# The prompt's compression units placed in the first sample pair's products, the head's constants in one transfer, and the instruction orders written anew

## The chip, the cores and the metric

The kernel runs on one core of a Trainium2 chip. The metric is the device time of one execution, in microseconds. The time before is the median of three runs. Beside them stands one profiled execution, from which every duration below is taken.

## The reference

One layer of a decoder is computed for a prompt group of 512 tokens and, with the same weights, for 8 decode samples of one token each, whose past of 1024 tokens lies in paged caches. Everything is float32.

```python
shift, scale, gate = jnp.split(jax.nn.silu(c) @ w_ada + b_ada, 3, axis=-1)
h = x * (1.0 + scale[:, None, :]) + shift[:, None, :]
parts = jnp.split(h @ w_in, np.cumsum(IN_WIDTHS)[:-1], axis=-1)
...
o_a = nsa_attention(...)    # compressed blocks, top-16 selected blocks, a window
o_b = moba_attention(...)   # top-3 past blocks by q . mean(k), and the own block
y_a = (o_a.reshape(bsz, t, NSA_WIDTH) * jax.nn.silu(a_z)) @ w_up_a
y_b = (o_b.reshape(bsz, t, MOBA_WIDTH) * jax.nn.silu(b_z)) @ w_up_b
mixed = (jax.nn.sigmoid(m_a) * y_a + jax.nn.sigmoid(m_b) * y_b) @ w_out
x_new = layer_norm(DEEPNORM_ALPHA * x + gate[:, None, :] * mixed, ln_g, ln_b)
```

The part that the change is about is the compression. Blocks of 32 rows, 16 apart, of the raw keys and values go with a position term through a small two-layer network, once for the prompt's own rows (31 blocks a head) and once for each sample's cache (63 blocks a head):

```python
def compress(kseq, pos_emb, w1, b1, w2, b2):
    ...
    blk = kseq[:, idx] + pos_emb[None, None, :, None, :]
    blk = blk.transpose(0, 1, 3, 2, 4).reshape(bsz, n, g, CMP_LEN * dh)
    return jax.nn.gelu(blk @ w1 + b1) @ w2 + b2
```

## The kernel before, in words

**Numbers.** Prompt and samples are handled together as 520 columns of transposed activations, in two halves of 260 (`HB`). Every float32 operand of a large product is split into a high and a low part of a reduced type, and each product is made of three: high by high, low weights by high, high weights by low. The high part is a cast on ACT, the low part a subtraction (`lo`, L367) on DVE or POOL. `LO_ENG` gives the turns of the two by three short patterns.

**The start.** SP issues all loads, at most eight in flight. `cT` (72 columns, the conditioning vectors), `bT` (16, the biases of shift and scale) and `cst` (141, small constants) are three transfers (L640 to L643). The eight blocks of `ada_ss`, the weights of shift and scale, come in 16 halves of 0.52 MB (`load_ada`, L565), and eight rows of x, 0.27 MB each (`load_x`, L550). Rows 0 to 3 go to buffers shared with later work (`ev`, `z`, `tmp`, `ev`), rows 4 to 7 to four buffers of their own (`xr`). For each row j, `ada` makes shift and scale on PE, and `ada_h` makes the modulated row: its high part `hTh` by one activation on ACT (512 columns) and its low part `hTl` by a multiply and a subtraction on DVE. The products of the first three groups of columns of w_in (`kc`, `vc`, `ks`, weights in `kd`, `v2`, `kl`) are added up row by row as the rows arrive (`early_mm`).

**The fills and the compression.** Then `dense` makes the other columns of w_in, 24 or 48 products of 260 columns for each half (`d<-hTh,hl` and `d<-hTl,hl`; the gates `ag` with weights of only 64 columns). Their weights pass through a ring: `raw` from memory, `hl` after the split. Between them stands the compression, `phis`. First comes `phi_prompt`: the prompt's own `kc` and `vc` rows are ordered into a tile `u` as 64 units with two columns of the position term behind them, and 48 products of 66 columns (`s<-u,w1h` and `s<-u,w1l`: 2 for keys and values, 8 slices, 3 parts) give the hidden layer, `gelu` follows, and `second` makes the second layer. Then `phi_pair` does the same for four pairs of samples, with 256 columns, from eight chunks `craw` of the cache, each of which is cast and subtracted into `u` (L1022 and L367). `u` has two buffers. What the network adds for the position term and bias, `cc`, is got from the last two columns of the prompt's products, so the prompt has to go through ahead of the first pair's `gelu`.

**What follows** is the same before and after but for its order: the decode samples' attention, the prompt's attention, the gates and up projections, the output projection, and the layer norm behind it.

**The order.** The program is traced in one order and then each engine's instructions are put into another one by `line_up`, from a table written out for each engine (`QUEUES`). A second set of tables (`SLOTS`) says for each pool which buffer the next tile gets. Nothing is decided by a scheduler at run time: an engine takes its next instruction and waits until its operands are there.

## Time and profile before

| | |
|---|---|
| runs | 604.09, 603.15, 602.0 us; median 603.15 |
| profiled execution | 605.51 us, of which the span of its trace is 603.8 |
| mean granted clock of PE in it | 0.991 |
| instructions of PE, DVE, ACT, POOL | 4721, 824, 688, 317 |
| bytes moved | 124.82 MB, mean 207 GB/s |
| chain that ended last | PE 79%, DVE 6%, DMA 5%, ACT 3%, POOL 2%, issue 2%, SP's queue 2% |

A row of the timeline has the start in us from the span's start, the duration, the engine, the line, the operation, "out<-in", the tile's shape, and how many like it follow one another ("x2"). In square brackets stands the idle time ahead of it and what ended that. Matmuls overlap, so the duration of one is longer than the distance from its start to the next start; the distance says what one costs. SPq is SP's queue of DMA issues; there the duration is that of issuing, with what holds up the issue. A row of the busy times by stretches has the stretch, its length, and for PE, PEld, DVE, ACT and POOL the busy time with the number of instructions, then the granted clock, the share of the DMA engines that was busy, and GB/s. A row of the groups has the count, the busy time and the mean ns of one, then the idle time ahead with its main releaser. PEld is the loading of weights, which overlaps PE.

### The profile page before, as it was taken

To read this page: it belongs to the slowest core of one execution; us is meant where nothing else is said; L and a number is where in the kernel's file an instruction comes from. 1 tells how busy PE (TensorE), PEld (TensorE's weight loads), DVE (VectorE), ACT (ScalarE), POOL (GpSimd) and SP (SyncE) were. 2 spreads that over 40 slices of the span, in tenths; PEclk is the share of its full clock that TensorE was granted. 3 is DMA by queue.
4 is the path that set the end of the run, shared out by engine and by line. 5 is a ranking of instruction groups with operands and counts; after the bars stand their busy time and mean duration, and the time that the engine had idled before them with its cause. 6 is when DMAs were issued, how large, how long until landed. Compare 5 with 4: busy or idle time off the path is not lost.

```text
span 603.8 us, 13227 instructions
## 1 busy us (share of the span) xinstructions
PE 588.1 (97%) x4721; PEld 504.0 (83%) x4721; DVE 293.2 (49%) x824; ACT 291.3 (48%) x688; POOL 271.5 (45%) x317
## 2 busy tenths in 40 slices
PE   7999999999999999999999999999999999999994
PEld 4789999999997888878768899987878697989773
DVE  1556534334374664644363545676421245334187
ACT  2457565635546546634446454575534134233343
POOL 0222567563433724351446728346361455354406
PEclk9998899999999999999999999999999999999998
DMA  8995465811665574466968635822997996332403
GB/s 300 401 362 169 111 195 162 277 36 36 185 183 166 186 246 144 161 234 240 370 226 324 246 122 197 279 104 57 325 399 245 374 347 222 106 117 89 188 1 141
DMA packets 63955, 124.82 MB, mean 207 GB/s; under 512 B 8402, under 2 KB 26258, under 8 KB 63378
## 3 DMA queue, kind: packets, MB, share of 16 engines
q1 hardware_dynamic: 62482, 119.79, 58.6%
q0 software_dynamic: 1408, 4.20, 1.8%
q8 instruction: 37, 0.61, 0.4%
q14 instruction: 28, 0.23, 0.1%
HBM read 114.37 MB, written 9.58 MB: 205 GB/s over the span
## 4 chain that ended last, share of the span: by engine, by line
PE 79%; DVE 6%; DMA 5%; ACT 3%; POOL 2%; issue 2%; SPq 2%; POOLq 0%; ACTq 0%; DVEq 0%
PE d L351 47%; PE s L351 12%; PE e L351 7%; PE o L351 5%; PE pt L354 5%; PE pt L351 2%; SPq L357 2%; DMA raw<-w_cols 2%; DMA u<-ada_ss 1%; DMA raw<-ada_g 1%; DVE bn L1762 1%; DMA raw<-mobv 1%; POOL p L1243 1%; DVE xt L1758 1%; POOL u L367 1%
## 5 line engine op out<-in xcount | busy, mean ns | idle before, releaser
L351 PE MATMUL d<-hTh,hl 128*128 128x260 f32 (+1 forms) x1392 | 266.4, 288 | 0.7 <-POOL hl L367 0.5
L351 PEld LDWEIGHTS d<-hTh,hl 128*128 128x128 f32 (+1 forms) x1392 | 217.1, 189 | 5.0 <-issue 1.7
L351 PE MATMUL d<-hTl,hl 128*128 128x260 f32 (+1 forms) x704 | 199.7, 284 | 0.0
L351 PEld LDWEIGHTS d<-hTl,hl 128*128 128x128 f32 (+1 forms) x704 | 132.5, 188 | 0.0
L367 POOL TENSOR_TENSOR hl<-raw,hl 128x512 fp32r<-128x512 f32 x57 | 77.3, 1356 | 113.8 <-ACT hl L447 91.4
L447 ACT CAST hl<-raw 128x512 fp32r<-128x512 f32 (+1 forms) x111 | 68.0, 617 | 51.4 <-PE d L351 43.9
L1241 ACT ACTIVATE p<-s,sm 128x256 f32<-128x256 f32 (+3 forms) x96 | 50.6, 529 | 71.5 <-DVE sm L1238 47.7
L1243 POOL TENSOR_SCALAR p<-p,sm,gp 128x512 f32<-128x512 f32 (+3 forms) x64 | 42.4, 670 | 70.8 <-DVE sm L1242 57.9
L367 DVE TENSOR_TENSOR hl<-raw,hl 128x512 fp32r<-128x512 f32 (+1 forms) x54 | 43.0, 800 | 40.8 <-ACT hl L447 37.8
L351 PE MATMUL d<-yh,hl 128*128 128x260 f32 x256 | 47.2, 285 | 0.0
L351 PEld LDWEIGHTS d<-yh,hl 128*128 128x128 f32 x256 | 39.9, 188 | 3.1 <-issue 1.7
L354 PE MATMUL pt<-cst,p 128*128 128x128 f32 x240 | 39.9, 279 | 0.6 <-POOL p L1243 0.6
L1243 POOL TENSOR_SCALAR p<-p,sm,cst 128x128 f32<-128x128 f32 (+3 forms) x32 | 20.9, 661 | 38.6 <-ACT pp L1251 16.4
L354 PEld LDWEIGHTS pt<-cst,p 128*128 128x128 f32 x240 | 27.2, 141 | 12.8 <-POOL p L1243 3.0
L351 PE MATMUL d<-yl,hl 128*128 128x260 f32 x128 | 36.3, 283 | 0.0
L1251 ACT COPY pp<-pt 128x512 f32<-128x512 f32 (+1 forms) x48 | 22.9, 478 | 27.0 <-PE pt L354 26.4
L351 PE MATMUL s<-u,w1h 128*128 128x256 f32 (+1 forms) x160 | 35.0, 287 | 0.6 <-POOL u L367 0.3
L1236 DVE TENSOR_REDUCE sm<-s 128x1 f32<-128x128 f32 (+1 forms) x48 | 16.8, 354 | 37.1 <-PE s L351 30.7
L1238 DVE CUSTOM_DVE_ANT_0 s<-s,band 128x256 f32<-128x256 f32 (+1 forms) x48 | 17.3, 365 | 34.5 <-PE s L351 24.7
L351 PE MATMUL s<-kd,q 128*128 128x256 f32 (+3 forms) x96 | 33.0, 348 | 0.2 <-ACT p L1241 0.2
L351 PE MATMUL s<-kd,qx 128*128 128x256 f32 (+3 forms) x96 | 30.6, 322 | 0.0
L351 PEld LDWEIGHTS s<-u,w1h 128*128 128x128 f32 x160 | 28.2, 198 | 1.2 <-POOL u L367 0.5
(413 smaller groups left out, 1044.8 us busy)
## 6 DMA issues: line engine op xcount, KB each, us to landing
raw<-w_cols SPq DMA_DIRECT2D x46, 512.0 KB, 6.0
raw<-mobk SPq DMA_DIRECT2D x64, 256.0 KB, 4.5
raw<-mobv SPq DMA_DIRECT2D x64, 256.0 KB, 5.3
craw<-cmp SPq DMA_DIRECT2D x64, 128.0 KB, 2.8
u<-ada_ss SPq DMA_DIRECT2D x12, 512.0 KB
raw<-slck SPq DMA_DIRECT2D x64, 64.0 KB, 3.0
raw<-ada_g SPq DMA_DIRECT2D x8, 512.0 KB, 5.5
raw<-w_up SPq DMA_DIRECT2D x8, 512.0 KB
```

What stands on the lines that cost most here:

```text
L351: return mmraw(out, lhsT, rhs, start=start, stop=stop, skip_group_check=True)
L354: return nc.tensor.transpose(out, x, unit)
L357: return nc.sync.dma_start(out, x)
L367: (nc.gpsimd if eng == "p" else nc.vector).tensor_sub(out, x, f32(hi))
L447: nc.scalar.copy(h, src)
L1236: nc.vector.tensor_reduce(sm[:, 0:1], s[:, :b], axis=AX, op=OP.min)
L1238: nc.vector.tensor_tensor_reduce(out=s[:, b:n], in0=s[:, b:n], in1=j.band[:, 256 - (n - b):], scale=1.0, scalar=top, op0=OP.add, op1=OP.mi ...
L1241: nc.scalar.activation(pr, s[:, :n], AF.Exp, scale=-1.0, bias=sm[:, 1:2], accum_out=sm[:, 2:3])
L1243: D.setdefault("pool", []).append(nc.gpsimd.tensor_scalar(pr, pr, sm[:, 3:4], j.gate(i), op0=OP.mult, op1=OP.mult))
L1251: j.copied[gi] = (nc.scalar.copy if COPY_ENG[gi] == "a" else nc.vector.tensor_copy)(t[:, :n], p[:, :n])
L1758: nc.vector.tensor_add(xt[tt][:, c], xt[tt][:, c], p)
L1762: nc.vector.bn_stats(BN[tt][0][:, BN[tt][1]], xt[tt][:, c0 + k:c0 + min(k + 256, n)])
```

## The change

1. **The ride.** The 64 units of the prompt and one column of the position term are put behind each half of the first pair's columns: of each slice of `u`, either half has 128 columns of the pair, 32 of the prompt and 1 of the position (`PAIR`). The 48 products of the pair are 322 columns wide, and the 48 products of 66 columns are gone. `gelu` is run once for all 322. In the second layer the three products for the keys are 320 wide, three for the prompt's values stay (64 columns of weights), and three products are gone. `phi_prompt` fills its columns of `u` ahead of the pair's cache pieces.
2. **The constants.** `cT`, `bT` and the first part of `cst` lie behind one another in one array, `first`, and come in one transfer to `first_in`.
3. **Row 0 of x** is modulated in two parts, columns 0 to 259 and 260 to 519, each with its own activation, multiply and subtraction.
4. **Rows 4 to 7 of x** go to the buffers of rows 0 to 3, so each of them waits until its predecessor has been read.
5. **Which engine subtracts** is given by two lists, one for the weights' ring (`HL_LO`), one for the rest (`LO`), in place of the three patterns.
6. **All orders**, `QUEUES` and `SLOTS`, are written anew.

The diff, without the tables but for a line or two:

```diff
+PAIR = 128 + 32 + 1
-LO_ENG = "dp", "pd", "dp"
+HL_LO = "dpdpdpdppdppdpddpdppdpdpdpdppdpdpdpdpdpdpdpdpdpdpdpdpdpdpdpdpdpdpdpdpdpdpdpdpdpdppddpdpdpdppdppddpdppddpdppddpd"
...
-    "phi.u": "01010010101010",
+    "phi.u": "010101010101",
...
-            eng = engs[0][turns[0] % len(engs[0])]
-            turns[0] += 1
+            eng = next(engs)
...
-                    lo(l, src, h)
+                    lo(l, src, h, next(hl_engs))
...
-        cst0 = per.tile([128, NC0], F32, name="cst0")
+        first_in = per.tile([128, 88 + NC0], F32, name="first_in")
+        cT, bT, cst0 = first_in[:, :72].rearrange("p (a b) -> p a b", a=8), first_in[:, 72:88], first_in[:, 88:]
...
-                if j < 4:
-                    xr[j] = row(*(("ev", 2), ("z", 1), ("tmp", 1), ("ev", 2))[j])
-                else:
-                    xr[j] = st.tile([128, NT], F32, name="xr", bufs=4)
+                xr[j] = row(*(("ev", 2), ("z", 1), ("tmp", 1), ("ev", 2))[j % 4])
...
-            D["act"] = nc.scalar.activation(hTh[:, j, :T], x[:, :T], AF.Identity, scale=s1[:, 0:1], bias=sh[:, 0:1])
+            if j:
+                D["act"] = nc.scalar.activation(hTh[:, j, :T], x[:, :T], AF.Identity, scale=s1[:, 0:1], bias=sh[:, 0:1])
+            else:
+                c = slice(0, HB)
+                nc.scalar.activation(hTh[:, j, c], x[:, c], AF.Identity, scale=s1[:, 0:1], bias=sh[:, 0:1])
+                nc.vector.tensor_scalar(h[:, c], x[:, c], s1[:, 0:1], sh[:, 0:1], op0=OP.mult, op1=OP.add)
+                nc.vector.tensor_sub(hTl[:, j, c], h[:, c], f32(hTh[:, j, c]))
+                c = slice(HB, T)
+                nc.scalar.activation(hTh[:, j, c], x[:, c], AF.Identity, scale=s1[:, 0:1], bias=sh[:, 0:1])
...
-        nc.sync.dma_start(cT, A["cT"])
+        nc.sync.dma_start(first_in, A["first"])
         load_ada(0)
-        nc.sync.dma_start(cst0, A["cst"][:, :NC0])
-        nc.sync.dma_start(bT, A["bT"])
...
-                        o = u[:, :n + 2] if n == 64 else u[:, :n]
-                        mm(o, wa[:, kv, l, :], r, l == 0 and j == 0, l == 7 and j == 2)
+                        mm(u[:, :n], wa[:, kv, l, :], r, l == 0 and j == 0, l == 7 and j == 2)
...
-                            cp(ut[kv][OWN[l2], x, :, g * 32:g * 32 + 32], v[OWN[g], :, :, l2])
+                            cp(ut[OWN[l2], x, :, g, 128:160], v[OWN[g], :, :, l2])
             yield 3000
-            gl = yield from units(64, lambda kv, x, l: ut[kv][:, x, l, :])
...
+            n = 16 * (PAIR if bp == 0 else 128)
+            uv = [u_tile(n=n) for _ in range(2)]
...
+            if bp == 0:
+                yield from phi_prompt(*kcvc, uv)
...
-            gl = yield from units(256, lambda kv, x, l: uv[kv][:, x, l * 256:l * 256 + 256])
+            n //= 8
+            gl = yield from units(n, lambda kv, x, l: uv[kv][:, x, l * n:l * n + n])
+            width = 320 if bp == 0 else 256
...
-                    mm(p[:, 0:256], wa[:, 0:128], gl[:, x], j == 0, j == 2)
+                    mm(p[:, 0:width], wa[:, 0:128], gl[:, x, :width], j == 0, j == 2)
...
-            second = yield from phi_prompt(*kcvc)
+            second = None
             for bp in range(4):
                 second = yield from phi_pair(bp, second)
```

What the new tables do is seen in the orders of the engines. The first place is SP's queue at the program's start, before (`ptt` is the page table, `raw<-w_cols` the weights of the first columns, `z`, `ev`, `tmp` take rows of x):

```order
L565 DMA u<-ada_ss 128x1024
L640 DMA cT<-cT 128x72
L565 DMA u<-ada_ss 128x1024 x3
L642 DMA cst_72<-cst 128x141
L550 DMA z<-xT 128x520
L643 DMA bT<-bT 128x16
L684 DMA ptt<-pt 1x64
L357 DMA raw<-w_cols 128x1024
L550 DMA ev<-xT 128x520
L357 DMA raw<-w_cols 128x1024
L565 DMA u<-ada_ss 128x1024 x2
L357 DMA raw<-w_cols 128x1024
```

And the same place now (`pt_103` is another form of the page table):

```order
L562 DMA u<-ada_ss 128x1024
L647 DMA first_in<-first 128x229
L562 DMA u<-ada_ss 128x1024 x3
L547 DMA ev<-xT 128x520
L359 DMA raw<-w_cols 128x1024 x2
L685 DMA pt_103<-pt 128x8
L689 DMA ptt<-pt 1x64
L547 DMA z<-xT 128x520
L562 DMA u<-ada_ss 128x1024 x2
L359 DMA raw<-w_cols 128x1024
```

Two weight tiles now stand seventh and eighth in the queue, directly behind the first row of x, where before `bT` and `ptt` stood ahead of the first of them.

The second place is SP's queue from the sixteenth to the thirtieth transfer, where the rows of x end, before:

```order
L565 DMA u<-ada_ss 128x1024
L550 DMA tmp<-xT 128x520
L565 DMA u<-ada_ss 128x1024
L550 DMA ev<-xT 128x520
L565 DMA y<-ada_ss 128x1024 x4
L550 DMA xr<-xT 128x520 x3
L565 DMA u<-ada_ss 128x1024 x4
```

And now, from the fifteenth to the twenty-eighth:

```order
L547 DMA tmp<-xT 128x520
L562 DMA u<-ada_ss 128x1024 x2
L562 DMA y<-ada_ss 128x1024
L547 DMA ev<-xT 128x520
L562 DMA y<-ada_ss 128x1024 x3
L547 DMA ev<-xT 128x520
L562 DMA u<-ada_ss 128x1024
L547 DMA z<-xT 128x520
L562 DMA u<-ada_ss 128x1024 x3
```

Rows 4 and 5, which take the buffers of rows 0 and 1, now stand among the last blocks of `ada_ss`, and rows 6 and 7 behind these.

The third place is PE in the fills, where the prompt's units stood before (`d<-hTh,hl 64x260` are the gates, `d<-cst_72,ev` transposes):

```order
L351 MATMUL s<-u,w1h 128x66
L351 MATMUL s<-u,w1l 128x66
L351 MATMUL s<-u,w1h 128x66
L351 MATMUL d<-hTh,hl 64x260
L351 MATMUL d<-hTl,hl 64x260
L351 MATMUL d<-hTh,hl 64x260
L351 MATMUL d<-hTl,hl 64x260
L351 MATMUL s<-u,w1h 128x66
L351 MATMUL s<-u,w1l 128x66
L351 MATMUL s<-u,w1h 128x66 x2
L351 MATMUL s<-u,w1l 128x66
L351 MATMUL s<-u,w1h 128x66
```

And PE now where the first of the pair's wide products stand:

```order
L353 MATMUL d<-hTh,hl 128x260 x2
L353 MATMUL d<-hTl,hl 128x260
L353 MATMUL d<-hTh,hl 128x260 x2
L353 MATMUL d<-hTl,hl 128x260
L356 MATMUL d<-first_in,ev 128x128 x4
L353 MATMUL s<-u,w1h 128x322
L353 MATMUL s<-u,w1l 128x322
L353 MATMUL s<-u,w1h 128x322 x2
L353 MATMUL s<-u,w1l 128x322
L353 MATMUL s<-u,w1h 128x322 x2
L353 MATMUL s<-u,w1l 128x322
L353 MATMUL s<-u,w1h 128x322 x2
```

The narrow products, which stood singly among gates and transposes, are gone; the wide ones stand in a block behind full products of 260 columns. Ahead of the first product of the first pair PE had 436 products, of which 252 had 128 rows of weights and 260 columns, and now has 412, of which 276 have.

## Prediction

> **What bounds the kernel now.** I read first the page's busy times and its slices, then the busy time by stretches, then the timeline of the start and of the two places where the compression's products stand.

> From the page, the span, the busy time of the engines, and the clock by slices of 15.1 us:

> ```profile
> span 603.8 us, 13227 instructions
> ...
> PE 588.1 (97%) x4721; PEld 504.0 (83%) x4721; DVE 293.2 (49%) x824; ACT 291.3 (48%) x688; POOL 271.5 (45%) x317
> ...
> PEclk9998899999999999999999999999999999999998
> ```

> PE is busy 97% of the span and the others half of it. The slices show a dip of the clock in the fourth and fifth. By stretches (columns: busy us of PE, PEld, DVE, ACT, POOL with counts, granted clock, DMA share, GB/s):

> ```profile
> 2.00:4.00 2.00, 1.18 (x3) 0.37 (x2) 0.00 (x0) 0.02 (x1) 0.00 (x0) 1.00 0.85 290
> 4.00:8.00 4.00, 2.65 (x12) 1.38 (x12) 0.44 (x2) 0.26 (x1) 0.00 (x0) 1.00 0.85 280
> 8.00:16.00 8.00, 6.96 (x50) 4.21 (x49) 2.84 (x12) 3.31 (x6) 0.00 (x0) 1.00 1.02 391
> 16.00:40.00 24.00, 23.85 (x232) 18.90 (x231) 12.55 (x39) 8.59 (x16) 4.11 (x3) 1.00 1.03 398
> ...
> 57.00:63.60 6.60, 6.60 (x34) 6.60 (x35) 2.00 (x6) 1.91 (x5) 0.00 (x0) 0.50 0.19 55
> 63.60:70.00 6.40, 6.40 (x55) 6.17 (x55) 3.97 (x10) 5.18 (x13) 3.90 (x4) 1.00 0.20 63
> ...
> 200.00:300.00 100.00, 99.28 (x791) 80.57 (x790) 51.38 (x188) 53.49 (x144) 40.22 (x50) 1.00 0.65 218
> ...
> 400.00:500.00 100.00, 99.85 (x810) 78.50 (x807) 43.23 (x118) 44.13 (x112) 46.22 (x51) 1.00 0.80 283
> ```

> Three things are to be seen. In the body PE idles 0.15 to 0.72 us in 100, so a product taken off PE there is taken off the end, and the tail behind the last product stays. From 57 to 63.6 us the clock is at half and PE gets through 34 products in 6.60 us, against 55 in 6.40 just after. And the transfers move 280 to 290 GB/s until 8 us, but 391 to 398 after it, at a full share: the start is paced by what the first 8 us fail to move, and by when PE gets its first operands. That start, in the timeline:

> ```profile
> 4.96 1.20 SPq L643 DMA_DIRECT2D bT<-bT  x1
> ...
> 11.52 0.17 DVE L654 TENSOR_SCALAR bT<-bT 128x8 f32<-128x8 f32 x1 [6.22 <-DMA bT<-bT]
> ...
> 12.69 0.62 ACT L619 CAST kd<-raw 128x512 fp32r<-128x512 f32 x1 [2.42 <-DMA raw<-w_cols]
> ...
> 14.86 0.59 PE L351 MATMUL d<-hTh,kd 128*128 128x260 f32 x2
> ```

> The small vector `bT`, issued at 4.96, is waited for until 11.52; the first weights, by the 2.42 us of idle time behind their name, until 12.69; the first product of use is at 14.86.

> **The change, part by part.** First the narrow products that go. Their rows in PE's timeline, at full clock, and the group of those with the high part of the weights:

> ```profile
> 56.10 0.39 PE L351 MATMUL s<-u,w1h 128*128 128x66 f32 x2
> ...
> 56.66 0.28 PE L351 MATMUL s<-u,w1l 128*128 128x66 f32 x1
> ```

> ```profile
> L351 PE MATMUL s<-u,w1h 128*128 128x66 f32 x32 | 7.7, 292 | 0.3 <-ACT u L983 0.3
> ```

> Five products start from 56.10 up to 56.66, the last not counted, which gives 0.112 us each. 32 such with the high part and half as many with the low part are 48: 48 x 0.112 = 5.4 us, on PE and so on the path. [...]

> What they become is 66 columns more in 48 products of 256 columns. No row has 322 columns; the nearest are 256, of the same operands, and 512, near the end:

> ```profile
> 73.06 0.40 PE L351 MATMUL s<-u,w1h 128*128 128x256 f32 x2
> 73.30 0.28 PE L351 MATMUL s<-u,w1l 128*128 128x256 f32 x1
> 73.42 0.40 PE L351 MATMUL s<-u,w1h 128*128 128x256 f32 x2
> ```

> ```profile
> 587.61 1.56 PE L351 MATMUL d<-m,kd 128*128 128x512 f32 x6
> 589.00 0.86 PE L351 MATMUL d<-m,v 128*128 128x512 f32 x3
> ```

> Three starts from 73.06 to 73.42 are 0.120 us each, six from 587.61 to 589.00 are 0.232. In proportion that is 0.44 ns a column, and 322 columns come to 0.149: 48 x 0.029 = 1.4 us more. Bounds: nothing, if a wider product still hides in its weight load, to 48 x 0.112 = 5.4 if it cost as much as 512. I take the proportion, since 322 lies much nearer to 256. The second stage loses three products, taken as dear as the narrow ones, 0.3 us, and three others grow by 64 columns, 0.1. ACT, DVE and POOL lose the short gelu of the prompt and have a longer one; they are at half load, and gelu's result is wanted by PE only in the next pair. Products together: -5.4 + 1.4 - 0.3 + 0.1 = -4.2 us.

> Second, the dip of the clock. It begins right behind the narrow products, and PE was not idle ahead of it:

> ```profile
> 54.69 0.30 PE L351 MATMUL s<-u,w1h 128*128 128x66 f32 x1 [0.27 <-ACT u L983]
> ```

> That 0.27 us is its one wait from 50 to 57 us. My reason for the dip is what PE does in that time: a product of 66 columns holds PE for 0.112 us and streams for 66 x 0.44 ns = 0.029, a quarter; one of 256 streams nearly all of its 0.120. A stretch mixed of narrow ones, transposes and half-width ones of the gates is the thinnest stream of the body. In the new order the gates stand among full products, and the first pair's 322-column ones come in a block of 32, so no stretch is so thin. The price: 34 products at the rate behind the dip (55 in 6.40) take 4.0 us, so 2.6 are lost; half of 6.60, if all went with the clock, is 3.3. I take 3.0, and nothing or 3.3 as bounds.

> Third, the start. Now one transfer brings `cT`, `bT` and the constants, and both first weight tiles are issued as seventh and eighth transfer, with no small one ahead that holds a place. What must have landed for the first product is 0.12 MB of constants, four halves of `ada_ss` of 0.52, one row of x of 0.27 and one weight tile of 0.52, 3.0 MB: at 0.395 MB a us from 2.1 us on it is there at 9.7. From the weights' cast at 12.69 to the product at 14.86 there were 2.2 us, of which the halved first row saves some; with 1.1 to 2.2 the product is at 10.8 to 11.9, at best 4.1 us earlier. The stage as a whole can't run ahead of its transfers: at 0.395 for the 6 us to 8 they would have moved 2.37 MB instead of 0.58 + 1.12, so they are 0.67 MB, or 1.7 us, ahead. But PE wasn't waiting for transfers alone at the stage's end, which I put at the first product of the next stage:

> ```profile
> 43.93 0.40 PE L351 MATMUL d<-hTh,hl 128*128 128x260 f32 x2
> ```

> Between the bounds of 1.7 and 4.1 I take the middle, 2.9. On SP four rows of x (4 to 7) now reuse the buffers of rows 0 to 3 and wait for DVE and ACT to have read them, with the last four halves of `ada_ss` queued around them. In before DVE reads row 2 for the last time in the first of these two rows, and the last four halves of `ada_ss` are issued in the second:

> ```profile
> 21.63 0.54 DVE L590 TENSOR_SCALAR h<-tmp,ssh 128x512 f32<-128x512 f32 x1
> ```

> ```profile
> 22.33 4.66 SPq L565 DMA_DIRECT2D u<-ada_ss  x4
> ```

> Row 6 takes row 2's buffer and now stands behind those four, at 27.0 by these rows, some 4.8 us after that read at 22.2, so I cost the wait at nothing. If that cover is gone, each us of that wait is a us of the start.

> Last, all else in the new order. The idle time in 100 us of body now goes from 0.15 to 0.72; four hundreds all like the worse or all like the better row make up to 1.3 us either way of what stands. I take nothing.

> The sum: -4.2 - 3.0 - 2.9 = -10.1 us. The profiled execution took 605.5 us, 603.8 of span and 1.7 around it, and would come to 595.4. The median of the three others was 603.15, 2.4 below it; the same gain gives **593.1 us**.

> **Rivals.** *The dip stays or comes back elsewhere.* Against my reason: I infer it from one dip. If the clock looks at something else, 3.0 us are not won: 596.1 us. [...] Chance 0.18.

> *The start gives little back.* For it: 398 GB/s at a full share from 16 to 40 us, so what PE begins earlier it may wait for later. Half of 1.7 us, 0.8, instead of 2.9: 595.2 us. Chance 0.16.

> *PE stands at the first wide product.* The ride makes the prompt's units wait for the pair's eight split cache pieces. In before these were cast and subtracted late:

> ```profile
> 60.73 0.62 ACT L1022 CAST u<-craw 128x512 fp32r<-128x512 f32 x1 [4.29 <-PE s L351]
> ```

> ```profile
> 70.36 3.00 POOL L367 TENSOR_TENSOR u<-craw,u 128x512 fp32r<-128x512 f32 x2 [1.90 <-ACT u L1022]
> ```

> ```profile
> 71.04 0.28 PE L351 MATMUL s<-u,w1h 128*128 128x256 f32 x1
> ```

> The last pieces were ready at 73.4. In the new order PE comes to its first wide product at 71.04 - 5.4 - 3.0 - 2.9, and 24 products of 260 columns more stand ahead of it, 24 x 0.120 = 2.9: at 62.6. All else on PE is queued behind it. Were the pieces ready no sooner than 73.4 + 2, PE would stand 12.8 us and the kernel end at 605.9, slower. It decides from a wait of 11.9 us on. Against: the pieces waited 4.29 us at 60.73 for the narrow products to release their buffers, and these are gone; ACT was busy 1.91 us of 6.60 there. Chance 0.04.

> **How the numbers follow.** My forecast has 0.58, the three rivals 0.18, 0.16 and 0.04, and 0.04 is left for two of them together with a worse order, near 600. The range: down, a start of 4.1 and wide products for nothing, 593.1 - 1.2 - 1.4, and 1.3 for the order: 589; up, the dip stays with the lower start and a worse order, 596.1 + 1.2 + 1.3, near 599. 0.3% of the time, about what a measurement of this kernel can tell from no change, is 1.8 us, so faster means below 601.3: all but the third rival and part of the rest.

> **What would show it.** PE has 48 products of 322 columns, starts 0.149 us apart, none of 66, and about 51 fewer in all. The clock shows no half before the end. The first product of use is near 11 to 12 us and the first `hl` product stage begins about 3 us sooner. PE's idle time before the first wide product is under 1 us, and the body's hundreds still idle under 0.8 us each. I am wrong if a half-clock stretch of 6.6 us stands anywhere in the body, if wide products start at 0.120 or over 0.17 apart, or if PE waits for `u` for several us.

## The result and the profile after

| | before | after |
|---|---|---|
| median | 603.88 us (14 runs, 601.57 to 606.46) | 607.11 us (14 runs, 604.7 to 609.8) |
| ratio to before | | 1.0059, 95% interval 1.0038 to 1.008 |
| span of the profiled execution | 603.8 us | 604.9 us |
| PE's idle time from 40 to 594 us | 2.6 us | 8.7 us |
| from the start of PE's last product to the end (the tail) | 8.8 us | 9.9 us |

The change makes the kernel slower by 0.6%, 3.2 us. Forecast were 593.1 us and a range of 589 to 599. Both kernels ran on the same chip. From the page after, the lines that answer to those of before:

```profile
span 604.9 us, 13101 instructions
...
PE 582.3 (96%) x4670; PEld 499.3 (83%) x4670; DVE 293.5 (49%) x824; ACT 291.1 (48%) x686; POOL 265.1 (44%) x312
...
PEclk9999899999999999999999999999999999999997
```

PE has 51 products fewer and is busy 5.8 us less, as meant, but the span of this pair of profiled executions is longer by 1.1. (At the median it is 3.2: the profiled execution of before, at 605.51 us, lies 1.6 above the median of its runs; why is seen in the part on the half clock.) The slices of the clock show one dip of one slice in the body where before had two. (Ahead of the first rise of the clock, near 9 to 11 us, none is on record, and the views print it as full.) By stretches (the columns as in the prediction):

```profile
40.00:60.00 20.00, 18.82 (x154) 18.18 (x153) 14.89 (x25) 18.95 (x38) 9.53 (x10) 1.00 0.49 164
60.00:80.00 20.00, 17.95 (x128) 17.87 (x129) 7.43 (x16) 8.29 (x19) 6.76 (x6) 0.91 0.72 215
400.00:500.00 100.00, 97.24 (x789) 77.04 (x789) 41.36 (x113) 42.68 (x107) 44.93 (x51) 1.00 0.89 307
```

Here are the losses: PE idles 1.18 and 2.05 us in the two stretches in which it comes to the first wide products, where before it idled 0.27 in both together, and 2.76 us from 400 to 500, where before it idled 0.15. These are 5.6 of the 6.1 us of idle time that came on top; from 80 to 400 us it is 0.9 more, behind 500 it is 0.4 less. From 40 to 60 us ACT is busy 18.95 of 20 us: it is the engine that is full there. In the timeline of the first place, the instructions of DVE, POOL and PE that bear on it, and SP's queue:

```profile
48.72 1.49 DVE L991 CAST u<-eh 64x256 fp32r<-64x256 f32 x4
...
56.49 3.22 DVE L991 CAST u<-eh 64x256 fp32r<-64x256 f32 x3
...
56.73 1.30 POOL L368 TENSOR_TENSOR hl<-raw,hl 128x512 fp32r<-128x512 f32 x1 [2.54 <-ACT hl L448]
...
58.17 1.30 POOL L368 TENSOR_TENSOR u<-craw,u 128x512 fp32r<-128x512 f32 x1
...
59.80 1.24 POOL L368 TENSOR_TENSOR u<-craw,u 128x512 fp32r<-128x512 f32 x1 [0.33 <-ACT u L1024]
...
59.84 4.41 SPq L359 DMA_DIRECT2D craw<-cmp  x8
59.84 1.74 DVE L368 TENSOR_TENSOR u<-craw,u 128x512 fp32r<-128x512 f32 x1
61.62 0.29 DVE L763 COPY vnew<-d 8x128 f32<-8x128 f32 x1
62.05 0.61 PE L356 MATMUL d<-first_in,ev 24*128 24x24 f32 x5 [2.79 <-DVE vnew L763]
```

Read it from the last row back. Five transposes of the gates wait 2.79 us on PE for `vnew`, a copy of 0.29 us out of a tile `d`. On DVE `vnew` stands behind three casts of the prompt's units, which take 3.22 us together where the four at 48.72 took 1.49, and behind a subtraction of 1.74 us. One by one the three take 0.38, 1.48 and 1.34 us: the first begins ahead of POOL's subtraction at 56.73, the other two behind the start of one. The new tables put these casts ahead of `vnew`. Behind that wait the clock is at half from 62.09 to 65.50 us. The wide products themselves come out as forecast:

```profile
70.45 0.46 PE L353 MATMUL s<-u,w1h 128*128 128x322 f32 x2
...
74.78 0.31 PE L353 MATMUL s<-u,w1l 128*128 128x322 f32 x1
74.93 0.31 PE L353 MATMUL s<-u,w1h 128*128 128x322 f32 x1
```

Thirty start from 70.45 up to 74.93, 0.149 us each. From 400 to 500 us three waits make up the idle time:

```profile
446.39 1.06 PE L353 MATMUL s<-raw,cs 128*32 128x512 f32 x8 [0.81 <-ACT p L1254]
...
453.71 0.44 PE L356 MATMUL pt<-first_in,p 128*128 128x128 f32 x2 [0.77 <-POOL p L1256]
...
492.56 0.39 PE L353 MATMUL d<-yl,hl 128*128 128x260 f32 x1 [0.98 <-DVE yl L368]
```

In each case the releaser's engine did other work first: ACT a cast of a weight, POOL a product of a gate, DVE a sum. For the third that is not shown to be the cause: with the sum moved, its wait stayed (`late_waits` below).

The start, in the timeline of after, and the rows of `cT` and of `ssh`, the sums of shift and scale, in that of before:

```profile
5.09 0.26 ACT L656 ACTIVATE sc<-first_in 128x72 f32<-128x72 f32 x1 [3.07 <-DMA first_in<-first]
...
12.48 0.18 DVE L579 TENSOR_TENSOR ssh<-s,first_in 128x20 f32<-128x20 f32 x1 [6.47 <-PE s L353]
...
14.74 0.59 PE L353 MATMUL d<-hTh,v 128*128 128x260 f32 x2
```

```profile
4.46 0.26 ACT L651 ACTIVATE sc<-cT 128x72 f32<-128x72 f32 x1 [2.44 <-DMA cT<-cT]
...
12.65 0.18 DVE L582 TENSOR_TENSOR ssh<-s,bT 128x20 f32<-128x20 f32 x1 [0.96 <-PE s L351]
```

The one transfer lands 0.6 us later than `cT` did, `bT` is no longer waited for, and DVE waits for PE's product `s` of shift and scale until 12.48, as it did before until 12.65, 1.1 us after the wait for `bT` had ended. The first product of use starts at 14.74, against 14.86.

### The profile page after: what moved, and what is told of

Read it like the earlier page. It is cut to its first block, busy times and chain, and to the rows that moved or that the text cites. A ratio compares the mean times of both kernels' runs of the same rounds, so it can differ in the third digit from the quotient of the medians.

```text
span 604.9 us, 13101 instructions
## 1 busy us (share of the span) xinstructions
PE 582.3 (96%) x4670; PEld 499.3 (83%) x4670; DVE 293.5 (49%) x824; ACT 291.1 (48%) x686; POOL 265.1 (44%) x312
## 5 line engine op out<-in xcount | busy, mean ns | idle before, releaser
L448 ACT CAST hl<-raw 128x512 fp32r<-128x512 f32 x111 | 67.5, 616 | 57.1 <-PE d L353 32.8
L1254 ACT ACTIVATE p<-s,sm 128x384 f32<-128x384 f32 (+3 forms) x96 | 50.5, 528 | 62.5 <-DVE sm L1251 46.1
L1256 POOL TENSOR_SCALAR p<-p,sm,gp 128x512 f32<-128x512 f32 (+3 forms) x64 | 41.1, 651 | 65.8 <-DVE sm L1255 41.7
L356 PE MATMUL pt<-first_in,p 128*128 128x128 f32 x240 | 39.9, 279 | 1.3 <-POOL p L1256 1.3
L356 PEld LDWEIGHTS pt<-first_in,p 128*128 128x128 f32 x240 | 27.1, 140 | 13.0 <-POOL p L1256 4.0
L1249 DVE TENSOR_REDUCE sm<-s 128x1 f32<-128x256 f32 (+1 forms) x48 | 17.0, 355 | 42.6 <-PE s L353 41.8
L353 PE MATMUL s<-u,w1h 128*128 128x256 f32 (+1 forms) x128 | 28.7, 293 | 0.6 <-ACT x L1050 0.4
L1256 POOL TENSOR_SCALAR p<-p,sm,first_in 128x384 f32<-128x384 f32 (+3 forms) x32 | 20.4, 646 | 20.0 <-DVE sm L1255 17.6
L353 PE MATMUL o<-pp,v 128*64 128x512 f32 (+3 forms) x192 | 28.9, 440 | 0.0
```

The costliest lines, as they stand in the source:

```text
L353: return mmraw(out, lhsT, rhs, start=start, stop=stop, skip_group_check=True)
L356: return nc.tensor.transpose(out, x, unit)
L448: nc.scalar.copy(h, src)
L1249: nc.vector.tensor_reduce(sm[:, 0:1], s[:, :b], axis=AX, op=OP.min)
L1254: nc.scalar.activation(pr, s[:, :n], AF.Exp, scale=-1.0, bias=sm[:, 1:2], accum_out=sm[:, 2:3])
L1256: D.setdefault("pool", []).append(nc.gpsimd.tensor_scalar(pr, pr, sm[:, 3:4], j.gate(i), op0=OP.mult, op1=OP.mult))
```

## The experiments

Each ratio below is to runs of the kernel before on the same chip. Where a trace is called ahead of after's or behind it, that is the time at which PE has the same number of products still to do, in the one trace less in the other.

### The wait at 62 us, the tail, and the narrow products

In `vnew_first` the copy goes ahead of the casts (DVE's order):

```diff
+L763 COPY vnew<-d 8x128
 L991 CAST u<-eh 64x8x32 x3
 L982 TENSOR_TENSOR u<-pos,u 128x16
 L368 TENSOR_TENSOR u<-craw,u 128x4x16x8
-L763 COPY vnew<-d 8x128
```

> The changed kernel with one instruction moved: on DVE the copy of vnew out of its PSUM buffer stands ahead of the three casts of the prompt's units, instead of five instructions later. Theory A (PE's wait of 2.8 us ahead of the gates' transposes comes from that copy, and the half clock behind it from the wait): the wait is gone, no half clock stands between 20 and 590 us, and the time falls by 2.8 + 1.7 (half of one window of 3.41) to 4.5, or up to 6.2 with two windows: from 607.1 to 601 to 603. Rival B (the wait is only passed on, to the first wide product, whose pieces of the cache were ready just then): PE waits there for u for 2 us or more, and the time falls by under 1.5 us. Rival C (the half clock has nothing to do with the wait): the wait is gone, the half clock stays, 604.3.

Measured: 608.38 us, ratio 1.0077 (1.0049 to 1.0105), span 604.9. The wait of 2.79 is gone, as is the half clock, and nothing is won: waits of 0.71 us at 62, 0.28 at 65, 0.24 and 0.50 at the wide products and 0.60 at 77 take their place. The timeline there:

```profile
59.34 1.27 POOL L368 TENSOR_TENSOR u<-craw,u 128x512 fp32r<-128x512 f32 x1
60.99 1.37 POOL L368 TENSOR_TENSOR u<-craw,u 128x512 fp32r<-128x512 f32 x1 [0.38 <-ACT u L1024]
62.73 5.39 SPq L359 DMA_DIRECT2D craw<-cmp  x8
...
66.64 1.76 ACT L1024 CAST u<-craw 128x512 fp32r<-128x512 f32 x3 [2.08 <-DMA craw<-cmp]
...
67.93 2.46 POOL L368 TENSOR_TENSOR u<-craw,u 128x512 fp32r<-128x512 f32 x2 [5.57 <-ACT u L1024]
...
70.45 0.56 PE L353 MATMUL s<-u,w1h 128*128 128x322 f32 x2 [0.50 <-POOL u L368]
```

The casts are still late, so the subtractions behind them are late (62.74), so the cache's buffers come free late, so SP loads the next pieces from 62.73 on instead of 59.84 (1.2 us of that is a later start of this execution), and ACT, POOL and PE wait one after the other. So the casts seem to be the cause, and `vnew` only the first to show it; `casts_early` and `mended2` below bear that out.

In `tail_before` PE's last 660 instructions, and those of the other engines that go with them, stand as in the kernel before; `vnew_tail` has both edits.

```diff
-QUEUES, from PE's 660th last instruction on: the changed kernel's
+QUEUES, from there on: the order of the kernel before
```

> The changed kernel with the order of before in its last part: from where PE has 660 instructions of its list left (at 488.8 us in both traces) PE, DVE, ACT, GpSimd and SP go by the old order and the old buffers. Theory A (the new order of the last part costs 1.2 us at 491 us, of which 0.9 are made up by the end of PE, and 1.1 us behind the last product): the time falls by 1.1 to 2.0 us, to 605 to 606, and the time from PE's last product to the end is 15.0 us instead of 16.0, counted from the first of its last group. Rival (that difference is chance between two executions): 607.1, within 0.5.

> Both edits together. If the two costs are separate, the gains add up: 4.5 + 1.5 = 6 us, 601. If what PE gains at 62 us is lost to a later wait for transfers, it is no better than the better one of the two alone.

Measured: 611.18 us, ratio 1.0124 (1.0091 to 1.0157), and 612.52, ratio 1.0142 (1.011 to 1.0174). Both slower than the changed kernel, against every expectation. The grafted piece makes waits of its own about the seam, where the two orders meet (0.87 and 1.39 us for a load of `raw`, 1.69 for `yl` in both). The tail is 8.5 us in both, as short as before's, but waits of PE ahead of it give the other engines time, so these two don't settle it.

`before_wide` is the kernel before with each of its 48 narrow products read four times over, as 264 columns:

```diff
-                        o = u[:, :n + 2] if n == 64 else u[:, :n]
+                        o = u[:, :n]
+                        if n == 64:
+                            o = u[:, :264].rearrange("p (a c) -> p a c", a=4)
+                            r = r[:, None, :].to_broadcast([128, 4, 66])
```

> The kernel before, with each of its 48 products of 66 columns made 264 columns wide by reading the same 66 columns four times; the output is unchanged. It asks what the clock looks at. My reason in the prediction (narrow products stream too little): the half clock of 6.8 us behind them is gone, and against before the time falls by 3.0 less 48 x 0.010 = 0.5, that is by 2.5 us. Rival (the clock looks at something else, for instance at waits): the half clock stays, and the time is 0.5 us longer.

Measured: 606.35 us, ratio 1.0023 (0.9996 to 1.005): no gain, where 2.5 us were expected. The half clock at 57 us was gone, but in this execution the clock rose to full only at 21.42 us, so the place was met in another phase. It doesn't settle the dip; the runs further down say more.

### Where the order can be mended

`casts_early` moves the three casts to 53 us and `vnew` ahead; `late_waits` mends the three waits between 400 and 500 us; `out_before` takes the output stage's order from before (PE's last 187 instructions); `all_mended` has all three.

```diff
 L368 TENSOR_TENSOR kd<-ev,kd 64x512
+L991 CAST u<-eh 64x8x32 x3
 L790 TENSOR_TENSOR ev<-d,ev 24x260
 ...
-L991 CAST u<-eh 64x8x32 x3
+L763 COPY vnew<-d 8x128
 ...
-L763 COPY vnew<-d 8x128
```

```diff
-L448 CAST hl<-raw 128x512
 L1254 ACTIVATE p,sm<-s,sm 128x256
+L448 CAST hl<-raw 128x512
 ...
-L819 TENSOR_TENSOR y<-y,tmp 128x512
-L818 COPY szs<-tmp 128x8
 L1256 TENSOR_SCALAR p<-p,sm,first_in 128x384
+L819 TENSOR_TENSOR y<-y,tmp 128x512
+L818 COPY szs<-tmp 128x8
 ...
-L1616 SCALAR_TENSOR_TENSOR y<-e,szs 128x4x8
 L368 TENSOR_TENSOR yl<-y,yh 128x512
 L368 TENSOR_TENSOR yl<-y,yh 128x3x8
+L1616 SCALAR_TENSOR_TENSOR y<-e,szs 128x4x8
```

> The changed kernel, with the three casts of the prompt's units that stood ahead of vnew on DVE moved forward to where DVE is free (behind the subtraction of kd, at 53 us), and vnew's copy ahead of the pieces. Theory A (what holds PE between 54 and 72 us is the chain prompt's casts, freed buffer, load of the next piece of the cache, its cast, its subtraction; the copy of vnew was one more wait beside it): with the casts done by 55 us the load that stood at 59.8 (62.7 with vnew moved alone) is issued before 59.5, PE has no wait over 0.5 us from 54 to 72 us, and its first product of 322 columns starts at 65 to 66.5 counted from a first dense product at 42.6, instead of 70.1. Rival B (the loads themselves, or ACT's casts, are the limit): that product starts at 68.5 or later, with waits for u or for loads of over 1.5 us in all.

> The changed kernel, with the three waits of PE of 0.8 to 1.0 us between 440 and 495 us taken on: on ACT the exponential of 256 columns goes ahead of the cast that waits for its weights, on GpSimd the scaling of 384 columns ahead of the gate product, on DVE two of the low parts yl ahead of the one that waits for PE. Theory A (these waits are of the order alone): the idle time from 400 to 500 us falls from 2.76 to under 0.8 us and PE's end comes 2 us sooner against its time at 400 us. Rival B (the transfers of mobv set the pace there): the idle time turns up as waits for raw<-mobv or elsewhere before 500 us, and PE's end stays within 0.5 us.

> The changed kernel, with the order of before for the output stage alone (the last 187 instructions of PE, 66 of DVE, 37 of ACT, 13 of SP). Theory (the new order of that stage costs 1.1 us behind the last product, since DVE begins its sums at 574.0 instead of 572.3): from the first product of PE's last group to the end of the span it is 15.0 us, as before, instead of 16.0, and PE's end is where it was. Rival: 16.0 stays.

> The three edits together. If the waits are separate and are what the change lost, the gains add up: 4 + 2 + 1 us, from 607.1 to about 600, below before (603.9). If one feeds the next, or the pace is set by transfers, it stays above 603.

Measured, in one execution of each of the first three: `casts_early` 605.14 us, span 603.4, 1.5 us ahead of after's trace at PE's end, though it started 1.35 us behind; at 57.02 it has waited 1.54 us for the gate's sum (L790), which now stands behind the casts, and from there to 83 us PE waits nowhere. `late_waits` 606.34 us; two of the three waits are gone, that for `yl` stayed at 0.98, the idle time from 400 to 500 us is 1.54 instead of 2.76, and from 434 us to the end 1.7 us are won. `out_before` 612.13 us: the piece makes a wait of 5.3 us at its seam with a half clock about it, so the time is inconclusive like that of the first graft; the tail is 8.9 us. `all_mended` 610.47 us, ratio 1.0084 (1.0052 to 1.0116): 3.5 us ahead of after's trace at 559 us, then 4.7 us of waiting at the same seam.

`mended2` has what held, and places the casts one by one; its DVE order (the moves on ACT and POOL are the first two of `late_waits`):

```diff
 L368 TENSOR_TENSOR kd<-ev,kd 64x512
+L991 CAST u<-eh 64x8x32
 L790 TENSOR_TENSOR ev<-d,ev 24x260
 L758 COPY v<-d 128x512
+L991 CAST u<-eh 64x8x32
 L368 TENSOR_TENSOR hl<-raw,hl 128x512
 L790 TENSOR_TENSOR ev<-d,ev 24x260
-L991 CAST u<-eh 64x8x32 x3
+L991 CAST u<-eh 64x8x32
+L763 COPY vnew<-d 8x128
```

> The changed kernel with its waits at 54 to 62 us and at 446 and 453 us mended by order alone: on DVE the prompt's casts go one by one between the instructions that PE waits for, and vnew ahead of the pieces; the exponential on ACT and the scaling on GpSimd go ahead as in the earlier edit. Theory (what the change lost are such waits): PE's idle time from 40 to 80 us falls from 3.2 to under 1.0 us and from 400 to 500 us from 2.8 to under 1.6, and the time falls by 2 of the one, 1.3 of the other and up to 1.6 of the half clock, 3.5 to 5 us, from 607.1 to 602 to 603.6, at or below before (603.9). Rival (the gain is lost again to transfers or to later waits): above 605.

Measured: 603.71 us, ratio 0.9991 (0.9963 to 1.0019), span 601.0: level with before, 3.4 us under the changed kernel (4.1 by the two ratios). Against after's trace it is even at 52.8 us, 3.38 us ahead at 72.8 and 3.88 ahead at PE's end. Of the 3.38 the half clock is 1.5: the products behind the wait, up to that place, take PE 10.79 us in after's trace and 9.32 in that of `casts_early`, without a wait in either. The rest is waits (2.2 us less of them, with PE 0.3 longer busy). So waits that order alone takes away, and the half clock behind one of them, put the changed kernel behind before. They are not all: from 40 to 590 us PE still idles 5.7 us, against 8.7 in after's trace and 2.6 before. The timeline of `mended2` also shows when the casts are slow:

```profile
52.40 1.76 POOL L368 TENSOR_TENSOR hl<-raw,hl 128x512 fp32r<-128x512 f32 x1
...
53.04 1.36 DVE L991 CAST u<-eh 64x256 fp32r<-64x256 f32 x1
...
55.37 0.36 DVE L991 CAST u<-eh 64x256 fp32r<-64x256 f32 x1
...
56.73 1.30 POOL L368 TENSOR_TENSOR hl<-raw,hl 128x512 fp32r<-128x512 f32 x1 [2.57 <-ACT hl L448]
56.93 1.43 DVE L991 CAST u<-eh 64x256 fp32r<-64x256 f32 x1
```

Three equal casts take 1.36, 0.36 and 1.43 us. The first and the third begin while POOL subtracts, and end 0.24 and 0.33 us after POOL has ended (54.16 and 58.03); the second has POOL idle beside it. By these three rows a cast that begins beside POOL's subtraction is held until that has ended.

`mended3` tests that, and the tail. Against `mended2`:

```diff
 L368 TENSOR_TENSOR kd<-ev,kd 64x512
-L991 CAST u<-eh 64x8x32
 L790 TENSOR_TENSOR ev<-d,ev 24x260
 L758 COPY v<-d 128x512
-L991 CAST u<-eh 64x8x32
+L991 CAST u<-eh 64x8x32 x2
 ...
-L1793 RECIPROCAL agg<-agg 128x1
 L1769 TENSOR_TENSOR xt<-xt,s 128x512
 ...
+L1793 RECIPROCAL agg<-agg 128x1
 L1768 TENSOR_TENSOR d<-d,gb 128x512
+L1769 TENSOR_TENSOR xt<-xt,d 128x512
 ...
-L1769 TENSOR_TENSOR xt<-xt,d 128x512
```

The reciprocal was moved because of this row of DVE in after's timeline, idle time in the middle of the stage whose end is late:

```profile
584.26 0.16 DVE L1793 RECIPROCAL agg<-agg 128x1 f32<-128x1 f32 x1 [1.54 <-ACT agg L1783]
```

> The changed kernel with the three moves of mended2 and two more, all on DVE. The cast that in mended2 ran from 53.04 to 54.40 us, beside a subtraction of POOL that ended at 54.16, goes behind the gate's sum and the copy of v, to about 55.4 us, where POOL idles. And at the output stage one reciprocal goes behind five other instructions of DVE, which in the changed kernel's trace stood behind it for 1.54 us of idle time at 584.26. Theory (a DVE cast is held until POOL's subtraction beside it has ended; the tail is 1.0 us longer because DVE falls behind in the output stage): the moved cast takes under 0.45 us, PE's wait of 0.74 us at 54.90 goes, the tail behind PE's last product falls from 9.9 to about 8.9 us, and the time is 1.0 to 1.7 us below mended2's, 602.0 to 602.7 us. Rival for the cast (the casts are slow by themselves at this place): it stays over 1 us wherever it stands. Rival for the tail (POOL's and ACT's last instructions set it, not DVE): the tail stays at 9.9 us and the time at mended2's.

Measured: 602.27 us, ratio 0.9979 (0.9955 to 1.0004), span 600.7. The timeline of DVE and POOL:

```profile
55.44 0.77 DVE L991 CAST u<-eh 64x256 fp32r<-64x256 f32 x2
...
57.05 1.28 POOL L368 TENSOR_TENSOR hl<-raw,hl 128x512 fp32r<-128x512 f32 x1 [2.55 <-DMA craw<-cmp]
...
57.41 1.16 DVE L991 CAST u<-eh 64x256 fp32r<-64x256 f32 x1
```

Two casts with POOL idle take 0.77 together, the third, beside POOL's subtraction, 1.16: it ends at 58.57, 0.24 behind the subtraction that began ahead of it (58.33), as in `mended2`, and the rival, that the casts are slow by themselves at this place, falls. (In `mended4` below, a cast that began 0.24 us ahead of POOL's subtraction took 0.39.) What holds the cast no trace shows. The wait of 0.74 became 0.45 and 0.28, not nothing, and from the first product of `dense` to its last one PE is less than 0.1 us faster than in `mended2`. The tail is 9.3 us (600.7 less 591.37), 0.6 of the 1.1 back: DVE's order is part of the tail, not shown to be all. The intervals of the two ratios overlap, so that `mended3` is faster than `mended2` is not shown by the times.

`mended4` went on in the same way. Against `mended3`:

```diff
-L991 CAST u<-eh 64x8x32 x2
-L368 TENSOR_TENSOR hl<-raw,hl 128x512
+L991 CAST u<-eh 64x8x32
+L368 TENSOR_TENSOR hl<-raw,hl 128x512
+L991 CAST u<-eh 64x8x32
 ...
+L1768 TENSOR_TENSOR d<-d,gb 128x512
 L1800 SCALAR_TENSOR_TENSOR xt<-xt,agg,o 128x512
-L1768 TENSOR_TENSOR d<-d,gb 128x512
 ...
-L1800 SCALAR_TENSOR_TENSOR xt<-xt,agg,o 128x512
 L1768 TENSOR_TENSOR d<-d,gb 128x256
 ...
-L1024 CAST u<-craw 128x4x16x8
 L789 COPY ev<-d 24x260
+L1024 CAST u<-craw 128x4x16x8
```

> mended3 with five more moves inside a few instructions of their place. On ACT the copy of a gate goes ahead of a cast of a cache piece (PE's wait of 0.45 us at 54.89 in mended3 hangs on it), and the second half of row 0's last activation directly behind the first. On DVE the subtraction of a weight goes ahead of the second of the moved casts (PE's wait of 0.28 at 56.99). In the output stage DVE takes the second-last sums of products before work that nobody waits for, and the last scaling of a finished row goes behind the last sums. Theory (these waits are a matter of DVE's order alone, and the tail still has 0.4 us over the kernel before's): both waits go, 0.6 to 0.7 us, the tail falls from 9.3 to about 9.0, and the time is 0.6 to 1.0 us below mended3's: 601.3 to 601.7 us, under the kernel before by 0.3 to 0.5%. Rival (what one wait gives up the next one takes, as with the first mending of this place): 602.3 us, as mended3.

Measured: 603.79 us, ratio 1.0009 (0.9986 to 1.0031), span 603.2: a miss. The two waits are gone and two others stand in their place, 0.21 us at 58.88 and 0.79 at 60.91, with a half clock from 61.63 to 65.04 behind them; the tail grew to 10.8 us. The rival (what one wait gives up the next one takes) had the mechanism right, and its time of 602.3 us was still too low.

### The start and the tail by themselves

`no_ada7` takes 1.05 MB out of the start's transfers:

```diff
-            ss[j] = ss["t"][:, j % 2]
-            for hf in range(2):
+            ss[j] = ss["t"][:, j % 2 if j < 7 else 0]
+            for hf in range(2 if j < 7 else 0):
```

> The changed kernel without the last two transfers of ada_ss (1.05 MB); block 7 of shift and scale is made from the weights of block 6, so that part of the result is another. Theory A (the start is paced by its transfers, which is why the earlier first product gave nothing back): 1.05 MB at 0.40 MB a us are 2.6 us, and the first dense product, at 42.6 us in the changed kernel, comes 2 to 2.6 us earlier. Rival B (PE's own work and waits from the first product on set the end of the start): under 0.7 us earlier.

Measured: 608.47 us. The first product of `dense` starts at 43.68 us against 42.57 in after's trace, and 42.21 to 44.23 in the other runs with this start: no earlier, though 1.05 MB at the 0.395 MB a us of before's start are 2.7 us. PE is busy 20.00 of the 20 us from 20 to 40. The stage is not paced by its transfers but by PE.

`tail60` takes before's order for PE's last 60 instructions:

```diff
-QUEUES, from PE's 60th last instruction on: the changed kernel's
+QUEUES, from there on: the order of the kernel before
```

> The changed kernel, with the order of before for the last 60 instructions of PE, 58 of DVE, 25 of ACT and 12 of SP, that is from about 575 us on. Theory A (the 1.1 us behind the last product come from the order of the sums on DVE in that time): the time from the start of PE's last product to the end of the span falls from 9.9 us to under 9.2 (8.9 before). Rival B (DVE is late because PE ends the first half of the output later, 574.0 instead of 572.3, which these last instructions don't change): it stays above 9.6.

Measured: 610.29 us, with a wait of PE of 2.7 us at the seam. The tail is 8.2 us, under the 9.2 that theory A named, but that wait stands just ahead of it and gives DVE time, so the run doesn't decide. All five runs with before's order in the tail have 8.2 to 8.9 us there, and those with the changed kernel's 9.9 to 10.0: the order is the likely cause, and not shown.

### The half clock near 57 us

`before_again`, `before_third` and `before_fourth` are the kernel before, unchanged; `wide_again` is `before_wide` once more.

> The kernel before once more, for a second trace. In the first one the clock was at half from 56.8 to 63.6 us. If that half clock belongs to the kernel (narrow products in every execution), it is there again at the same place, for one or two windows of 3.41 us. If it depends on where the clock's windows fall in this execution, it may be gone, and the execution is then up to 3 us shorter than 605.5 us; the clock's first rise then comes at another time than 9.02 us.

> The kernel before, unchanged, to see how often its half clock near 57 us appears. Theory that the narrow products make it: half clock at 56 to 64 us again, 3 us lost against the first look's stretch ahead of it. Rival (it depends on where the clock's windows of 3.41 us fall in this execution): present or absent as it happens, in a trace whose first rise of the clock stands at another time.

> The kernel before, unchanged, a fourth look, with the same two expectations as before_third: by the theory of the narrow products a half clock at 56 to 64 us; by the rival present or absent as it happens.

> The kernel before with its 48 products of 66 columns read four times over, as 264 columns, once more. If narrow products make the half clock near 57 us, it is absent in this look as in the first. If it is chance, it may stand there, and one such look is enough to end the theory.

Measured:

| trace | first rise of the clock | half clock in the body | time |
|---|---|---|---|
| before, first profiled execution | 9.02 us | 56.81 to 63.64 | 605.51 us |
| before_fourth | 9.32 | 57.11 to 63.93 | 605.29 |
| before_again | 14.46 (its start is 3.2 us late) | none | 605.28 |
| before_third | 11.45 | none | 603.14 |
| wide_again | 8.96 | none | 605.02 |

The changes of the clock in a trace stand a whole number of 3.413 us apart: from 9.02 to 56.81 are 14 of them, as from 9.32 to 57.11, the half clock of before is two of them long (6.83 us), and that of the changed kernel one (3.41). Below, these steps of 3.413 us, counted from a trace's own changes, are called windows; their phase differs from execution to execution. Take the window ahead of the drop, and those that other traces have at the thinnest place; groups of products that start in it (each view begins 0.27 to 0.28 us behind the window's start, which leaves out products that began ahead of it), first in the first profiled execution of before (53.39 to 56.81 us):

```profile
L351 PE MATMUL s<-u,w1h 128*128 128x66 f32 x14 | 2.9, 276 | 0.3 <-ACT u L983 0.3
L351 PE MATMUL s<-u,w1l 128*128 128x66 f32 x7 | 1.9, 276 | 0.0
L351 PE MATMUL d<-hTh,hl 128*64 128x260 f32 x3 | 0.8, 291 | 0.0
L351 PE MATMUL d<-hTl,hl 128*64 128x260 f32 x3 | 0.8, 281 | 0.0
```

The same groups in `before_third`, 55.82 to 59.23 us, its thinnest window:

```profile
L351 PE MATMUL s<-u,w1h 128*128 128x66 f32 x14 | 2.7, 260 | 0.0
L351 PE MATMUL s<-u,w1l 128*128 128x66 f32 x7 | 1.9, 276 | 0.0
L351 PE MATMUL d<-hTl,hl 128*64 128x260 f32 x5 | 1.3, 282 | 0.0
L351 PE MATMUL d<-hTh,hl 128*64 128x260 f32 x4 | 1.1, 298 | 0.0
L354 PE MATMUL d<-cst,ev 128*104 128x128 f32 x1 | 0.3, 317 | 0.0
```

And in the changed kernel, 58.68 to 62.09 us, the window with the wait:

```profile
L353 PE MATMUL d<-hTh,hl 128*128 128x260 f32 x2 | 0.4, 282 | 0.0
L353 PE MATMUL d<-hTl,hl 128*128 128x260 f32 x1 | 0.3, 283 | 0.0
```

At 0.44 ns a column (estimated from products of 256 and 512 columns, whose starts are 0.120 and 0.232 us apart), the first window streams 21 x 66 + 6 x 260 = 2946 columns, 1.30 of its 3.41 us or 0.38; the second 3854 columns, 0.50; the third 780, 0.10. Worked out so for all traces of this case, the windows in the body behind which the clock falls have 0.00 to 0.17 (seven, each with a wait of PE), 0.38, 0.39 (the kernel before, twice) 0.42 (`mended4`), and one 0.60 (`vnew_tail`, at 490 us); of those behind which it stays full, one has 0.42 and all others 0.47 or more. The 0.60 is the exception: nearly nine tenths of it are eight products whose weights fill 32 of 128 columns, in two groups of four that start within 0.02 us. Counting each group once gives it 0.20, but then windows of that kind at full clock come as low as 0.25 (the kernel before at 486.9 us), so the columns streamed are not the whole measure. In the first windows after the rise, between 11 and 18 us, it stayed full at 0.31 to 0.43 too, so what was seen holds for the body. `wide_again`, whose windows begin 0.07 us from those of the first profiled execution of before, has the same stretch at 0.87 and no drop.

So a thin stream goes with the drop, as the prediction had it, but only where a window falls on it: in two of four traces of the kernel before. The changed kernel's wait shows the same: in `out_before` PE waits 2.80 us for `vnew` as in after's trace, but a window's end falls into the wait, the two windows have 0.42 and 0.52, and the clock stays full. What the dip costs is read from traces of one and the same program. `before_third` is 0.42 us behind the first profiled execution at 54.7 us and 2.70 ahead at 67, a difference of 3.12; `before_again` goes from 3.21 behind to 0.09, again 3.12.

How often it comes, the mean granted clock of the runs tells roughly. It is 0.991 in both traces of before with the dip and 0.995 and 0.996 in those without. Of the 80 executions of before that were timed beside the experiments, 54 have 0.995 to 0.997, with a median of 603.0 us, and 26 have 0.987 to 0.993, with a median of 606.6. So about two thirds of them, and the median with them, seem to have no dip. Of the 14 runs of the changed kernel nine have 0.992 or less; its profiled execution, with a half clock, has 0.991, and `casts_early` and `mended2`, which have none in the body, have 0.994. The mean doesn't place the dip: four of the twelve runs of `before_wide` have 0.990 to 0.993 too, with no longer times than its others.

## Why the prediction was wrong, by its own steps

The terms of the sum, from one profiled execution to the other:

| term | forecast | measured |
|---|---|---|
| products | -4.2 us | -4.2 |
| dip of the clock | -3.0 | -1.6 |
| start (PE's idle time up to 40 us) | -2.9 | -0.2 |
| "all else in the new order" | 0 | +6.1 idle, +1.1 tail |
| sum | -10.1 | +1.2; the spans differ by +1.1 |

**Products: right.** Starts are 0.149 us apart, as forecast. PE's busy time fell by 5.8 us, of which 1.6 is the clock.

**The dip: its place and the thin stream that goes with it right, the size wrong twice.** Its price of 3.0 was 3.1. But the step that gave the median of three the same gain as the profiled execution counted a dip that two of four traces don't have, and by their clocks some two thirds of the runs: the 2.4 us by which that median lay below the profiled execution is most of the dip's price. And the changed kernel has one of its own: the window at half clock behind the 2.79 us wait, worth 1.5 us. No narrow products are left, but the window with that wait streams in only 0.10 of its time.

**The start: wrong.** The step failed that put the first product at the landing of the transfers and 1.1 to 2.2 us more. It left out PE's own product of shift and scale, on which `ssh` and with it the modulated row wait. That wait ended last before too, at 12.65 against 11.52 for `bT`; with `bT` gone it ends at 12.48, 0.2 us earlier. And "the stage as a whole can't run ahead of its transfers" took the transfers for the pace; `no_ada7` shows that it is PE's. The first product of `dense` starts 1.4 us earlier, but with 12 products fewer ahead of it, 12 x 0.120 = 1.4 us: next to nothing is won.

**"Last, all else in the new order ... I take nothing": the step that decided.** The bound of 1.3 us either way was taken from the idle time of before, that is, from another order. The new one idles 6.1 us more. `mended2` shows that order makes half of it: moving a handful of instructions on three engines, with every product and transfer as in the changed kernel, takes 3.0 us of the idle time and the half clock away and recovers 3.4 us at the median. The other 3.1 us of idle time no run took away; whether they are order too, or come with the ride or the shared buffers, stays open. The tail, which the prediction said "stays", is 1.1 us longer, of which DVE's order in `mended3` accounts for 0.6; the grafts that should have isolated the rest made waits of their own, so the rest stays open.

**The rival named the place and had the wrong wait.** "PE stands at the first wide product" had PE waiting for the pair's pieces. It stood 8 us ahead of them, at the gates' transposes, behind the prompt's casts, which share DVE with both. `vnew_first` shows the rival's own wait as soon as the first is taken away: 0.24 and 0.50 us at the wide products, through buffers of the cache that come free late. The first wide product started at 70.08, not 62.6; in `mended3`, with the waits mostly gone, at 67.03.

Of the signs that the prediction named, the products' count and pitch, and the missing narrow ones, held; "no half before the end", "near 11 to 12 us", "about 3 us sooner", "under 1 us" ahead of the first wide product (3.2 from 40 us on) and "under 0.8 us each" failed.

## What to carry to other kernels

When all orders are written anew, the order is a term of its own and not noise: its bound is not the idle time of the old order, and the first thing to find out is which short instruction that PE needs now stands behind long ones on another engine. A wait that was mended there came back one step later (in `vnew_first` 2.79 us as five of 0.24 to 0.71, in `mended4` 0.45 and 0.28 as 0.21 and 0.79), so follow the chain to the slow instruction at its root, here casts of 0.36 to 0.39 us that took 1.16 to 1.48 beside another engine's subtraction. And before a dip of the clock goes into a sum, see whether the kernel has it in every execution: a profiled execution that is slower than the median is a hint that it doesn't (here 605.51 us against 603.15).
